# All rows behind the convolution turned by VectorE and DRAM in a two-layer streaming encoder

## The chip, the cores and the metric

The kernel runs on one core of a Trainium2 chip. The core has TensorE (PE in the profile, with its weight loads as PEld), VectorE (DVE), ScalarE (ACT), GpSimd (POOL) and SyncE (SP), which here issues the DMAs. The metric is the time of one execution on the device in microseconds (us), as the median of several runs. Instructions of one engine run in the order that was fixed when the program was built; engines wait for each other through semaphores.

## The reference: what is computed

The input is 256 rows (time steps) of 1024 float32 channels, h below. There are two layers. Each is a macaron: half a SwiGLU feed-forward network (FFN), a mixer, half an FFN again, each added to h; a last RMSNorm follows. The mixer of the first layer is a convolution module, that of the second is latent attention. What matters here is the end of the convolution and the FFN behind it:

```python
u = a * jax.nn.sigmoid(b)                  # a, b: the two halves of h @ w_pw1
u = causal_depthwise_conv(u, w_dw)         # 31 taps for each channel
u = jax.nn.silu(rmsnorm(u, g_norm))
h = h + u @ w_pw2                          # 1024 x 1024: "the last products"
h = h + 0.5 * swiglu_ffn(rmsnorm(h, ffn_norm2[0]), w1, w3, w2)
```

## The kernel before, in words

**Tiles and blocks.** The 256 rows are two row blocks tb of 128; the 1024 channels are eight tiles k or f of 128. Weights come in blocks of 1 MB, 128 x 2048 float32, in the order of use. Each is loaded into one of three raw buffers by SP (`load`, lines 162 to 192, and `raw_to`, line 156, which issues loads ahead without casting). It is then split in two pieces of 128 x 1024 each: ACT writes the high part `hi` (line 188), DVE the rest `lo` (line 189), both in the rounded format that TensorE multiplies fast. Five pairs of `hi` and `lo` buffers exist. A product of high precision is three products: high by low, high by high, low by high (`mm3`, lines 272 to 278). The stationary operand of a product is a tile of activations with the channels on the partitions, so h, which lies with the rows on the partitions, has to be turned, scaled by the gain of the norm and split into `Xh` and `Xl` ahead of each FFN. The factor of the norm itself is applied behind the product.

**Two ways of turning.** In the first, TensorE transposes 128 x 128 squares into PSUM, four at a time (`transposed`, line 315), ACT scales them into `Xh` (line 333) and DVE makes `Xl` (line 337); `Norm.part` (line 382) calls it. In the second, `turn_blocks` (line 345) lets DVE transpose the 32 x 32 blocks of 128 x 512 values, SP writes them to DRAM with four DMAs and reads them back with one, and `Norm.columns` (line 430) makes `Xh` and `Xl` from what came back:

```python
last_turn[0] = nc.vector.transpose(t[:, :w], src.rearrange("p (t j q) -> p j t q", t=n, q=32))
d = dram.tile([P, w], F32, tag=tag + "d", name=uid(tag + "d"), bufs=4)
dv = d.rearrange("(j p) (i c) -> i p j c", p=32, c=32 * n)
for i in range(4):
    dma = nc.sync.dma_start(dv[i], t[32 * i:32 * i + 32, :w].rearrange("p (j c) -> p j c", j=4))
...
last_read[0] = nc.sync.dma_start(b[:, :w], d)
```

A `Norm` made with `turn_by_dma` takes the second way for its second row block: `begin` (line 416) issues the turns of h[1], `end` (line 443) the columns, and the FFN starts with `first_chunk` (line 678), whose products go in the order: first half of the chunk for row block 0 (24 products), four k of the second half for row block 0 (12), first half for row block 1 (24), then the rest. The norm behind the convolution is made without it and takes the first way for all 16 squares.

**The end of the convolution** (`conv_in`, from line 776). The tap sums of the last two channel tiles are finished by DVE, ACT and POOL; `ends` (line 993) adds them and squares them (ACT); TensorE sums the squares over the channels; `normed` (line 938) makes the factor (ACT, then POOL's power), spreads it by a small product `rb`, and then for five groups of tiles makes z (DVE, line 954, lists `zs`), `Zh` (ACT, line 958, `zhs`) and `Zl` (DVE, line 960, `zls`). For each list, entries 0 to 4 (or 0 to 7 for `zs`) belong to row block 0 and the rest to row block 1. The last products (`mm`, line 1031) run over tb, then f, then the two output halves d of 512 columns; behind each tb the outputs are added to h (`add`, line 1078, DVE). h[0] is turned by TensorE between the products of tb 1 (line 1114), h[1] between the first products of the FFN (line 1122).

**What sets the order.** A planner orders each engine's instructions by priority and by a simulated time line. `urgent` raises the priority of what a function issues. `order(a, b)` puts a behind b, without a wait on data. `casts[n, i]` are the two casts of piece i of block n; `n_used[0]` is at this place the index of the first weight block of the next FFN. `turns` holds the reads of turned rows; a weight load that is issued later is put behind the last of them (line 183).

Of the kernel before, what the change touches and what calls it, by code (L numbers as in the profile page):

```python
# [23 lines left out]
KT = D // P  # L24
# [15 lines left out]
RAW_BUFS = 3  # L40
W_BUFS = 5
WARM = 21
PIECES = 2
# [41 lines left out]
def trunk(ctx: ExitStack, tc: tile.TileContext, x, xt, first, pos, invf, gfin, wdw,  # L85
# [27 lines left out]
    conv_block = {}  # L113
# [18 lines left out]
    loaded = []  # L132
    n_used = [0]
# [3 lines left out]
    def order(ins, first):  # L137
        tc.add_manual_dep(ins.ins, first.name, mybir.DependencyInfo(
            mybir.DependencyClass.NoSync, mybir.DependencyReason.DATA), reason="order")
# [7 lines left out]
    casts = {}  # L147

    turns = []
    last_read = [None]  # L150
    last_turn = [None]
# [4 lines left out]
    def raw_to(last):  # L156
        while len(loaded) + len(raws) < last:
            src = blocks[len(loaded) + len(raws)]
            raw = rawp.tile([P, HB], F32, tag="raw", name=uid("raw"))
            raws[len(loaded) + len(raws)] = raw, nc.sync.dma_start(raw[:, :src.shape[-1]], src)  # L160
# [66 lines left out]
    h = [const.tile([P, D], F32, name=f"h{tb}") for tb in range(NT)]  # L227
# [15 lines left out]
    for k in range(KT):  # L243
        c = slice(k % 4 * 512, k % 4 * 512 + 512)
# [42 lines left out]
    def tbs(tb):  # L287
        return slice(tb * P, (tb + 1) * P)
# [56 lines left out]
    def turn_blocks(pool, src, n, tag, after=()):  # L345


        w = n * P
        t = pool.tile([P, 512], F32, tag=tag + "t", name=uid(tag + "t"), bufs=2)
# [5 lines that stand above are left out]
            for a in after:  # L355
                order(dma, a.ins)
        b = pool.tile([P, 512], F32, tag=tag + "b", name=uid(tag + "b"), bufs=2)
        last_read[0] = nc.sync.dma_start(b[:, :w], d)
        return b[:, :w].rearrange("p (i t q) -> p t i q", i=4, q=32)

    class Norm:


        def __init__(self, gname, half=False, turn_by_dma=None):
            self.col = GCOL[gname]
            self.half = half

            self.pool = turn_by_dma
            self.turning = []

            self.first_ahead = False
            self.whole = False
            self.xh = xp.tile([P, KT, S], F32R, tag="Xh", name=uid("Xh"))
            self.xl = xp.tile([P, KT, S], F32R, tag="Xl", name=uid("Xl"))
            self.r = [None] * NT
            self.rh = [None] * NT
            self.turned = ()
            self.lows, self.highs = [], []

            self.between = None  # L380
# [34 lines left out]
        @urgent  # L415
        def begin(self):

            raw_to(len(loaded) + RAW_BUFS)
            first = [dma for raw, dma in raws.values()]
            for q in range(2):  # L420
                self.turning.append(turn_blocks(self.pool, h[1][:, 512 * q:512 * q + 512], 4, "h", first))
                first = [last_read[0]]
                turns.extend(first)
                if self.first_ahead and q == 0:
                    order(last_turn[0], self.lows[3].ins)
                    for low in self.lows[4:]:
                        order(low, last_turn[0].ins)
# [165 lines left out]
    class Rows:  # L593
# [4 lines left out]
        def mm(self, part, i, tb, d, o, f0, f1, o0=0, o1=512, after=(), after_last=()):  # L598
            hi, lo = part
            for j in range(2):  # L600
                f = 2 * i + j
                c = slice(j * D + d * 512 + o0, j * D + d * 512 + o1)
                mm = mm3(o, self.zh[:, f, tbs(tb)], self.zl[:, f, tbs(tb)], hi[:, c], lo[:, c], f == f0,
                         f == f1 - 1, [*after, *after_last] if j else after)
            return mm
# [166 lines left out]
    def conv(X, make_next):  # L772
        with tc.tile_pool(name="conv", bufs=1) as act:
            return conv_in(act, X, make_next)

    def conv_in(act, X, make_next):
# [49 lines left out]
        mm = None  # L826
        for n, (i, tb) in enumerate(CONV_STEPS):
            t = every if tb is None else tbs(tb)
            load_to(conv_block[CONV_TILES[min(CONV_TILES.index(i) + 2, KT - 1)]] + 1)
            gate, u = bank("A", "gate"), bank("A", "u")  # L830
            mm = products(i, 1, t, gate, mm)
            if n == 1:
                X.late((mm,))
                mm = X.turned[-1]
            mm = products(i, 0, t, u, mm)
# [19 lines left out]
        mm = products(7, 1, tbs(1), last_gate, mm)  # L855
# [3 lines left out]
        mm = pairs(mm)  # L859
# [57 lines left out]
        sq = {}  # L917

        def square(k, t):
            if k not in sq:  # L920
                sq[k] = act.tile([P, S], F32, tag="sq", name=uid("sq"), bufs=8)
            return nc.scalar.activation(sq[k][:, t], Y[:, k, t], AF.Square)
# [11 lines left out]
        zs, zhs, zls, norms = [], [], [], []  # L934
# [58 lines left out]
        def ends(tb, after):  # L993

            t = tbs(tb)

            @urgent
            def add():
                for k in CONV_LAST:
                    if CONV_HALVES[k, tb] < TAPS:  # L1000
                        last = nc.vector.tensor_add(Y[:, k, t], part[k][:, t], Y[:, k, t])
                        order(last, dve_ends[-1].ins if tb == 0 else dve_last[-4 if k == CONV_LAST[0] else -1].ins)
                        if tb == 0:
                            firsts_of["add"] = last
                        elif k == CONV_LAST[1]:

                            order(zls[4], last.ins)
                    firsts_of["sq"] = square(k, t)
                sums[tb] = sums_of(tb, CONV_LAST, after)

            add()
# [19 lines left out]
        def mm(f, tb, d, kinds="lhx"):  # L1031
            w = loaded[conv_block[-1 - f // 2]]
            c = slice(f % 2 * D + d * 512, f % 2 * D + d * 512 + 512)
            hi, lo = w
            for n, kind in enumerate(kinds):
                p = nc.tensor.matmul(o[tb, d], (Zl if kind == "x" else Zh)[:, f, tbs(tb)],  # L1036
                                     (lo if kind == "l" else hi)[:, c], start=(f, kind) == (0, "l"),
                                     stop=(f, kind) == (KT - 1, "x"))
                if kind == "l":
                    firsts.append(p)  # L1040
            return p
# [15 lines left out]

        for ins in dve_first[-4:]:
            order(ins, firsts_of["add"].ins)
        order(prods_last[-16], firsts_of["sq"].ins)  # L1060
        ms_ins, power = norms[0]
        order(power, pool_last[-22].ins)
        for ins in pool_last[-21:]:
# [13 lines left out]
        @urgent  # L1077
        def add(tb, d):
            c = slice(d * 512, d * 512 + 512)
            last = nc.vector.tensor_add(h[tb][:, c], o[tb, d], h[tb][:, c])  # L1080
            if tb == 0:
                order(last, zls[7].ins)

        nxt = None
        n_used[0] = max(conv_block.values()) + 1
# [1 line left out]
        for tb in range(NT):  # L1087
            for d in range(2 * tb):
                o[tb, d] = bank("A", "o")
            for f in range(KT):  # L1090
                firsts.clear()

                for kinds in ("lhx",) if f > 1 else ("x",) if (tb, f) == (0, 0) else ("lh", "x"):
                    now = [mm(f, tb, d, kinds) for d in range(2)]
                if tb == 0 and f == 1:
                    sums_of(1, early[5:], now[1])
                elif tb == 0 and f == 5:
                    then = now[1]
                elif tb == 0 and f == 6:

                    ends(1, then)
                    for p in firsts:
                        order(p, sums[1].ins)
                    normed(1, (now[1],))
                elif tb == 0 and f == 7:
                    for p in firsts:
                        order(p, brow[1].ins)

                    for i in range(PIECES):
                        hi, lo = casts[max(conv_block.values()) + 1, i]  # L1110
                        order(hi, zhs[7].ins)
                        order(lo, zs[-1].ins)
                if tb == 1 and f in (2, 4):
                    nxt.part(0, f // 2 - 1, (now[1],))
                if tb == 1 and f == 4:
                    nxt.rms(0)
            for d in range(2):
                add(tb, d)
            if nxt is None:
                nxt = make_next(act)  # L1120
                nxt.between = []
        nxt.part(1, 0)
        return nxt


# [342 lines left out]
    X = ffn(X, lambda act: Plain("mix_0", act), beside)  # L1468
    for _ in todo:
        pass  # L1470
    X = conv(X, lambda act: Norm("ffn2_0", half=True))
    apart.close()
    X = ffn(X, lambda act: Norm("ffn1_1", half=True, turn_by_dma=rows), apart=True)
    X = ffn(X, lambda act: Norm("mix_1", turn_by_dma=rows), apart=True)
# [99 lines left out]
```

## Time and profile before

| | |
|---|---|
| median of 3 runs | 917.44 us (917.42 to 917.92) |
| the profiled execution's own time | 916.85 us |
| its span, first to last instruction | 915.0 us |
| granted TensorE clock, mean | 0.999 |
| DVE busy, ACT busy | 593.0 us (65%), 494.7 us (54%) |
| q1, SP's DMAs | 194.32 MB, 61.5% of 16 DMA engines' span |
| end of the convolution to the next FFN's second chunk | from 265.86 to 300.59 us of the span |

How to read it: times in the profile count from the first instruction of the span. A line of the time line has the start, the length, the engine, the line of the kernel, the operation, what is written and read (buffer numbers left out), the shape and the number of instructions merged in it; in square brackets stands the idle time before it and what ended that. Busy time of TensorE is modelled from pipelined products whose lengths overlap, so the distance between two starts says more than a length.

### The profile page before, as it was taken

Reading aid. Unit: us, or ns where it says so; the run is one execution under the profiler, and the core shown is the slowest. Engines: PE = TensorE matmul, PEld = TensorE weight load, DVE = VectorE, ACT = ScalarE, POOL = GpSimd, SP = SyncE. Lnnn points to the kernel's source line nnn. Section 1 sums busy time; section 2 is a strip of 40 time slices with the busy share of each in tenths; the row PEclk is TensorE's granted clock in tenths of the full one; section 3 lists DMA queues with packets and bytes.
Section 4 is the critical chain, followed back from the end, with each engine's and each line's share of the span. In section 5 each row is a group of like instructions: output and inputs, shape, how many; then the busy total and the mean of one; then the engine's idle time right before and its main releaser. Section 6 shows DMA issues by size and latency. Waiting matters only on the chain.

```text
span 915.0 us, 12095 instructions
## 1 busy us (share of the span) xinstructions
PE 908.0 (99%) x4329; PEld 764.0 (83%) x4329; DVE 593.0 (65%) x934; ACT 494.7 (54%) x845; POOL 125.8 (14%) x259
## 2 busy tenths in 40 slices
PE   9999999999999999999999999999999999999997
PEld 7888888898988888888888888888898888888886
DVE  6885764489987666654476666545768577566633
ACT  7654544388877444543374544433677564454432
POOL 1730000079941000000010000000400010000000
PEclk9999999999999999999999999999999999999999
DMA  9987776533227766776568777755445378776711
GB/s 338 319 290 257 254 275 226 187 140 138 93 79 272 247 230 236 248 232 225 196 208 283 249 246 241 238 205 159 167 145 184 140 250 301 242 245 223 254 47 47
DMA packets 66732, 195.78 MB, mean 214 GB/s; under 512 B 11888, under 2 KB 38384, under 8 KB 47344
## 3 DMA queue, kind: packets, MB, share of 16 engines
q1 hardware_dynamic: 66240, 194.32, 61.5%
q8 instruction: 34, 0.56, 0.2%
q10 hardware_dynamic: 432, 0.69, 0.2%
q14 instruction: 26, 0.21, 0.1%
HBM read 180.30 MB, written 14.68 MB: 213 GB/s over the span
## 4 chain that ended last, share of the span: by engine, by line
PE 99%; DMA 0%; ACT 0%; SPq 0%; DVE 0%; issue 0%; ACTq 0%
PE u L274 17%; PE u L278 17%; PE u L277 17%; PE o L278 10%; PE o L274 10%; PE o L277 10%; PE u L801 3%; PE gate L801 3%; PE o L1036 2%; PE u L283 2%; PE tp L318 1%; PE pairs L844 1%; PE a L277 1%; PE a L274 1%; PE a L278 1%; PE nope L277 1%
## 5 line engine op out<-in xcount | busy, mean ns | idle before, releaser
L189 DVE TENSOR_TENSOR lo<-raw,hi 128x1024 fp32r<-128x1024 f32 (+1 forms) x292 | 344.4, 1220 | 177.2 <-ACT hi L188 176.6
L188 ACT CAST hi<-raw 128x1024 fp32r<-128x1024 f32 x294 | 292.1, 1046 | 241.7 <-PE o L278 81.9
L274 PE MATMUL u<-lo,Xh 128*128 128x512 f32 x672 | 261.7, 389 | 0.0
L278 PE MATMUL u<-hi,Xl 128*128 128x512 f32 x672 | 261.6, 389 | 0.0
L277 PE MATMUL u<-hi,Xh 128*128 128x512 f32 x672 | 261.5, 389 | 0.0
L278 PEld LDWEIGHTS u<-hi,Xl 128*128 128x128 f32 x672 | 126.1, 188 | 26.8 <-DVE Xl L337 0.5
L277 PEld LDWEIGHTS u<-hi,Xh 128*128 128x128 f32 x672 | 126.1, 188 | 26.0
L274 PEld LDWEIGHTS u<-lo,Xh 128*128 128x128 f32 x672 | 126.1, 188 | 26.0
L278 PE MATMUL o<-hi,Gl 128*128 128x512 f32 (+1 forms) x356 | 137.7, 387 | 0.0
L277 PE MATMUL o<-hi,Gh 128*128 128x512 f32 (+1 forms) x356 | 137.7, 387 | 0.0
L274 PE MATMUL o<-lo,Gh 128*128 128x512 f32 (+1 forms) x356 | 137.3, 387 | 0.0
L309 POOL TENSOR_TENSOR ms<-ss 128x1 f32<-128x1 f32 x16 | 9.4, 589 | 590.7 <-ACT junk L301 590.7
L278 PEld LDWEIGHTS o<-hi,Gl 128*128 128x128 f32 x356 | 66.8, 188 | 13.6
L277 PEld LDWEIGHTS o<-hi,Gh 128*128 128x128 f32 x356 | 66.9, 188 | 13.5
L274 PEld LDWEIGHTS o<-lo,Gh 128*128 128x128 f32 x356 | 66.9, 188 | 13.5
L675 ACT CAST Gh<-gb 128x512 fp32r<-128x512 f32 (+1 forms) x48 | 28.0, 583 | 70.8 <-DMA gb<-gd 70.8
L676 DVE TENSOR_TENSOR Gl<-gb,Gh 128x512 fp32r<-128x512 f32 (+1 forms) x48 | 31.3, 652 | 53.5 <-ACT Gh L675 53.5
L890 DVE SCALAR_TENSOR_TENSOR acc<-V,dw,acc 128x128 f32<-128x128 f32 (+1 forms) x174 | 53.9, 392 | 0.0
L911 ACT ACTIVATE prod<-V,dw 128x128 f32<-128x128 f32 (+1 forms) x128 | 45.6, 415 | 1.9 <-POOL Y L912 1.0
L763 DVE TENSOR_TENSOR s<-s,u 128x512 f32<-128x512 f32 (+1 forms) x48 | 30.5, 635 | 7.9 <-PE u L278 7.9
L762 ACT ACTIVATE s<-u,R 128x512 f32<-128x512 f32 (+1 forms) x48 | 31.1, 649 | 4.6 <-PE u L278 3.9
L350 DVE STREAM_TRANSPOSE gt<-s 128x512 f32<-128x512 f32 (+1 forms) x48 | 32.0, 666 | 1.4
(225 smaller groups left out, 884.8 us busy)
## 6 DMA issues: line engine op xcount, KB each, us to landing
raw<-in_f2w SPq DMA_DIRECT2D x66, 1024.0 KB, 5.0
raw<-in_f1w SPq DMA_DIRECT2D x62, 1024.0 KB, 5.1
raw<-in_cw SPq DMA_DIRECT2D x12, 1024.0 KB, 4.8
gd<-gt SPq DMA_DIRECT2D x160, 64.0 KB, 3.3
gb<-gd SPq DMA_DIRECT2D x40, 256.0 KB, 4.4
raw<-in_wo SPq DMA_DIRECT2D x4, 1024.0 KB, 4.8
raw<-in_wuq SPq DMA_DIRECT2D x3, 1024.0 KB, 4.8
raw<-in_f1w SPq DMA_DIRECT2D x8, 256.0 KB, 4.7
```

What stands on the lines that cost most here:

```text
L188: casts[len(loaded), i] = (nc.scalar.copy(hi[:, c], raw[:, c]), low.tensor_sub(lo[:, c], raw[:, c], hi[:, c].bitcast(F32)))
L189: low.tensor_sub(lo[:, c], raw[:, c], hi[:, c].bitcast(F32)))
L274: mm = nc.tensor.matmul(o, ah, bl, start=start, stop=False)
L277: nc.tensor.matmul(o, ah, bh, start=False, stop=False)
L278: return nc.tensor.matmul(o, al, bh, start=False, stop=stop)
L350: last_turn[0] = nc.vector.transpose(t[:, :w], src.rearrange("p (t j q) -> p j t q", t=n, q=32))
L676: nc.vector.tensor_sub(Gl[:, f, tbs(tb)].rearrange("p t (i q) -> p t i q", q=32), bv, gh.bitcast(F32))
L762: nc.scalar.activation(s[:, :w], u[0, tb][:, :w], AF.Silu, scale=X.r[tb])
L763: nc.vector.tensor_mul(s[:, :w], s[:, :w], u[0, tb][:, w:] if both else u[1, tb])
L801: mm = nc.tensor.matmul(u[:, t], w[:, c], X.x[:, k, t], start=(k == 0), stop=(k == KT - 1))
L890: dve_last.append(nc.vector.scalar_tensor_tensor(out if j == j1 - 1 else y, v, w, y, op0=ALU.mult, op1=ALU.add))
L911: prods_last.append(nc.scalar.activation(p, v, AF.Copy, scale=w))
```

## The change

The norm behind the convolution is made with `turn_by_dma`, so none of its rows are turned by TensorE. h[0] is added and turned as soon as each output of tb 0 is there, in a stated order between DVE's other work; `Norm.both` marks this norm, and for it `begin` issues only one weight load ahead, behind the reads of h[0], and puts the low parts of h[0] behind the turns of h[1]. The last products of tb 1 go over f 0 to 3 for both outputs, then f 4 to 7 for output 0, then f 4 to 7 for output 1. The two high casts of the first weight block of the next FFN are put behind the first square and behind the factor's first step of row block 1, its first low cast in front of z, its second behind the last `Zl`.

```diff
@@ class Norm, __init__
+            self.both = False
@@ class Norm, begin
-            raw_to(len(loaded) + RAW_BUFS)
+            raw_to(len(loaded) + (1 if self.both else RAW_BUFS))
             first = [dma for raw, dma in raws.values()]
+            if self.both:
+                for dma in first:
+                    order(dma, turns[-1].ins)
             for q in range(2):
                 self.turning.append(turn_blocks(self.pool, h[1][:, 512 * q:512 * q + 512], 4, "h", first))
                 first = [last_read[0]]
                 turns.extend(first)
+                if self.both:
+                    for low in self.first_lows[q]:
+                        order(low, last_turn[0].ins)
@@ conv_in, ends: firsts_of["sq"] becomes a list of the two squares
-                    firsts_of["sq"] = square(k, t)
+                    firsts_of.setdefault("sq", []).append(square(k, t))
...
-        order(prods_last[-16], firsts_of["sq"].ins)
+        order(prods_last[-16], firsts_of["sq"][1].ins)
@@ conv_in, add
             if tb == 0:
-                order(last, zls[7].ins)
+                order(last, (zls[6], zs[-1])[d].ins)
+                nxt.first_turns.append(turn_blocks(nxt.pool, h[0][:, c], 4, "h"))
+                turns.append(last_read[0])
+                for ins in ((zls[7], zs[-4]), zls[8:])[d]:
+                    order(ins, last_turn[0].ins)
@@ conv_in, the last products
-            for f in range(KT):
+            halves_of = [(f, (0, 1)) for f in range(KT - 4 * tb)]
+            halves_of += [(f, (d,)) for d in range(2 * tb) for f in range(KT - 4, KT)]
+            for f, ds in halves_of:
                 firsts.clear()
                 for kinds in ("lhx",) if f > 1 else ("x",) if (tb, f) == (0, 0) else ("lh", "x"):
-                    now = [mm(f, tb, d, kinds) for d in range(2)]
+                    now = [mm(f, tb, d, kinds) for d in ds]
+                if ds == (1,):
+                    for p in firsts:
+                        order(p, half_done.ins)
+                if tb == 1 and f == KT - 1:
+                    add(1, ds[0])
+                    half_done = now[0]
...
+                    (hi, lo), (hi2, lo2) = (casts[n_used[0], i] for i in range(PIECES))
+                    order(hi, firsts_of["sq"][0].ins)
+                    order(firsts_of["sq"][1], hi.ins)
+                    order(hi2, norms[1][0].ins)
+                    order(zhs[5], hi2.ins)
+                    order(lo, zls[4].ins)
+                    order(zs[8], lo.ins)
+                    order(lo2, zls[9].ins)
                     for i in range(PIECES):
-                        hi, lo = casts[max(conv_block.values()) + 1, i]
-                        order(hi, zhs[7].ins)
-                        order(lo, zs[-1].ins)
-                if tb == 1 and f in (2, 4):
-                    nxt.part(0, f // 2 - 1, (now[1],))
-                if tb == 1 and f == 4:
-                    nxt.rms(0)
-            for d in range(2):
-                add(tb, d)
-            if nxt is None:
+                        hi, lo = casts[n_used[0] + 1, i]
+                        order(hi, zhs[9].ins)
+                        order(lo, lo2.ins)
+            if tb == 0:
                 nxt = make_next(act)
-                nxt.between = []
-        nxt.part(1, 0)
+                nxt.both = True
+                nxt.first_turns, nxt.first_lows = [], [[], []]
+                for d in range(2):
+                    add(0, d)
+                for q in range(2):
+                    for high, low in nxt.columns(nxt.first_turns[q], q, 0):
+                        order(high, casts[n_used[0] + 2, PIECES - 1][0].ins)
+                        order(low, casts[n_used[0] + 1, PIECES - 1][1].ins)
+                        nxt.first_lows[q].append(low)
+                    if q == 1:
+                        for i in range(PIECES):
+                            order(casts[n_used[0] + 2, i][1], low.ins)
+                nxt.rms(0)
@@ trunk
-    X = conv(X, lambda act: Norm("ffn2_0", half=True))
+    X = conv(X, lambda act: Norm("ffn2_0", half=True, turn_by_dma=rows))
```

More of the change, by code (lines that the diff above doesn't have):

```diff
@@ L995, in ends @@
             t = tbs(tb)
+            firsts_of["sq"] = []
             @urgent
```

## The prediction

> **What bounds the kernel now.** I read the page first: the span, the busy time of TensorE (PE) and the shares of the chain that ended last.
>
> ```profile
> span 915.0 us, 12095 instructions
> PE 908.0 (99%) x4329; PEld 764.0 (83%) x4329; DVE 593.0 (65%) x934; ACT 494.7 (54%) x845; POOL 125.8 (14%) x259
> PE 99%; DMA 0%; ACT 0%; SPq 0%; DVE 0%; issue 0%; ACTq 0%
> ```
>
> TensorE is the bound from end to end; nothing else holds a share of the chain. So only two things count: how much PE time the change takes out, and whether PE is made to wait anywhere. I went next to the timeline of PE from the first product of the convolution's second row block (265.86) to the first product of the next FFN's second chunk (300.59).
>
> ```profile
> 265.86 0.39 PE L1036 MATMUL o<-lo,Zh 128*128 128x512 f32 x1
> ...
> 271.12 0.39 PE L1036 MATMUL o<-hi,Zl 128*128 128x512 f32 x1
> 271.35 0.60 PE L318 MATMUL tp<-ident,h 128*128 128x128 f32 x4
> 271.70 0.47 PE L1036 MATMUL o<-lo,Zh 128*128 128x512 f32 x1
> ...
> 280.62 0.39 PE L278 MATMUL u<-hi,Xl 128*128 128x512 f32 x1
> ...
> 300.59 0.39 PE L274 MATMUL u<-lo,Xh 128*128 128x512 f32 x1
> ```
>
> ```profile
> L318 PE MATMUL tp<-ident,h 128*128 128x128 f32 x16 | 2.4, 276 | 0.0
> L1080 DVE TENSOR_TENSOR h<-o,h 128x512 f32<-128x512 f32 x4 | 2.6, 680 | 0.0
> ```
>
> The durations overlap, so the starts are what to read. From 265.86 to 271.12 lie 23 steps, 0.2287 us each; from 280.62 to 300.59 lie 88, 0.2269 us each. Four transposes push the next product from 271.35 to 271.70, though the row gives each 276 ns.
>
> **What the change takes off PE.** The stretch is 300.59 - 265.86 = 34.73 us and holds 48 products of the convolution, 96 of the FFN and the 16 transposes of h. Without the transposes, and with every operand there in time, it is 48 x 0.2287 + 96 x 0.2269 = 10.98 + 21.78 = 32.76. So 1.97 us is all there is to win (0.123 us for each transpose, a short wait for h included). Doing the last products output by output only reorders them and costs PE nothing.
>
> The rest of the sum is whether the rows come in time over the longer way: an add and a 32x32 turn on VectorE (DVE), four DMAs to DRAM, one back, then the scaled high part on ScalarE (ACT) and the low part on DVE. I name the four next weight blocks B0 to B3 and start the FFN at 265.86 + 10.98 = 276.84.
>
> **The moved casts.** B0's casts now stand in front of and between the convolution's last copies.
>
> ```profile
> 262.10 0.31 ACT L922 ACTIVATE sq<-Y 128x128 f32<-128x128 f32 x1 [1.18 <-DVE Y L1001]
> 265.05 0.31 ACT L958 ACTIVATE Zh<-z 128x128 fp32r<-128x128 f32 x1 [1.84 <-DVE z L954]
> 264.67 1.12 DVE L954 SCALAR_TENSOR_TENSOR z<-Y,G,rb 128x128 f32<-128x128 f32 x4 [2.26 <-PE rb L947]
> 265.71 0.58 DVE L960 TENSOR_TENSOR Zl<-z,Zh 128x128 fp32r<-128x128 f32 x2
> 266.20 1.12 DVE L954 SCALAR_TENSOR_TENSOR z<-Y,G,rb 128x128 f32<-128x128 f32 x4
> 268.77 2.35 DVE L189 TENSOR_TENSOR lo<-raw,hi 128x1024 fp32r<-128x1024 f32 x2
> 271.04 0.75 DVE L960 TENSOR_TENSOR Zl<-z,Zh 128x256 fp32r<-128x256 f32 x2
> 271.15 28.00 SPq L180 DMA_DIRECT2D raw<-in_f2w  x8
> 272.73 1.99 ACT L188 CAST hi<-raw 128x1024 fp32r<-128x1024 f32 x2
> ```
>
> The two waits of ACT (1.18 and 1.84) each take one high cast of 1.99 / 2 = 1.0, and DVE's 2.26 takes one low cast of 2.35 / 2 = 1.18. All three go at nothing; without that cover each would be added to the norm on which PE waits. If the first cast ran 0.2 us over its wait, the square and the norm behind it would be late by that much, but PE then has products of the first row block to do, so up to about 0.3 us stays hidden.
>
> **DVE's own order.** After the second low part of Z (265.71 + 0.58 = 266.29) it has to do: add 0.68, turn 0.71, four scalings 1.12, a low part 0.4, add 0.68, turn 0.71, two low parts 0.75, B0's second low cast 1.18, B1's two 2.35. That is 8.58, so 274.9 at the latest; consecutive rows overlap by 0.05 us (266.20 begins before 266.29), which makes it about 274.5. Z's low parts move by about a microsecond (the third from 267.7 to 268.9), and PE wants that one 16 steps behind 265.86, at 269.5: still in time. The first turn ends at 267.6, the second at 270.3.
>
> The durations of the turn and the new low and high parts are those of the same code in the next FFN:
>
> ```profile
> 451.81 0.71 DVE L350 STREAM_TRANSPOSE rows<-h 128x512 f32<-128x512 f32 x1
> 465.10 1.24 DVE L439 SCALAR_TENSOR_TENSOR Xl<-rows,G,Xh 128x128 fp32r<-128x128 f32 x4 [0.16 <-ACT Xh L438]
> 464.66 1.28 ACT L438 ACTIVATE Xh<-rows,G 128x128 fp32r<-128x128 f32 x4 [0.73 <-DMA rows<-hd]
> ```
>
> The four old Xh and Xl groups go, four new ones of 1.28 and 1.24 come; DVE gains four turns (2.84 us), which its idle time behind 276 holds.
>
> **The DRAM trips.** SyncE (SP) issues in order, so a read that waits for its writes holds what is behind it. The same trips stand in the trace:
>
> ```profile
> 451.14 0.33 SPq L160 DMA_DIRECT2D raw<-in_f1w  x1
> 452.55 1.75 SPq L354 DMA_DIRECT2D hd<-rows  x4
> 457.20 0.34 SPq L358 DMA_DIRECT2D rows<-hd  x1
> 457.64 1.83 SPq L354 DMA_DIRECT2D hd<-rows  x4
> 461.21 0.34 SPq L358 DMA_DIRECT2D rows<-hd  x1
> 462.46 1.84 SPq L354 DMA_DIRECT2D hd<-rows  x4
> 465.70 0.34 SPq L358 DMA_DIRECT2D rows<-hd  x1
> 468.31 1.28 ACT L438 ACTIVATE Xh<-rows,G 128x128 fp32r<-128x128 f32 x4 [1.79 <-DMA rows<-hd]
> 641.43 1.75 SPq L354 DMA_DIRECT2D hd<-rows  x4
> 645.76 0.34 SPq L358 DMA_DIRECT2D rows<-hd  x1
> ```
>
> From first write to read: 3.24 (462.46), 3.57 right behind another read (457.64), 4.33 (641.43), 4.65 with a weight load 1.4 us ahead (452.55; 6.06 from that load). From read to ACT's start: 2.61 (465.70 to 468.31) to 3.45 (461.21 to 464.66). The DMA engines are free when the change begins to use them (columns of the view by stages: busy PE, PEld, DVE, ACT, POOL, then clock, DMA share, GB/s):
>
> ```profile
> 268.00:270.00 2.00, 2.00 (x11) 1.63 (x10) 2.00 (x4) 2.00 (x6) 0.00 (x0) 1.00 0.04 8
> 270.00:272.00 2.00, 2.00 (x12) 1.69 (x11) 2.00 (x4) 2.00 (x4) 0.00 (x0) 1.00 0.00 0
> ```
>
> So: h0's first half writes 267.6, reads 270.8, reaches ACT at 273.5 to 274. ACT has B2's high casts before it, which end at 272.73 + 1.99 = 274.7 in the old order and hardly earlier in the new one, since the same product frees their buffer; so it starts at about 275. PE wants the first column at 276.84. Margin over 1 us. Second half: writes 271.2, reads 274.8, ACT at 277.5 to 278.2; wanted at 276.84 + 12 x 0.2269 = 279.56. Margin 1 us. B3's load follows at 275.2 (in the old order loads began at 271.15). h1's first half: its last product starts at 276.84 - 13 x 0.2287 = 273.9 and ends 0.39 later, DVE is free at 274.6, add and turn end at 276.0, the writes queue behind B3, the read comes 6.06 after that load at 281.2, ACT at 284.0; wanted after 36 products at 285.0. Second half: writes 281.6, reads 285.2 (3.57), ACT 287.8 (2.61), first column 0.3 later at 288.1; wanted after 48 products at 287.7. **This is the tight place.** With the quickest rows throughout (3.24 each) it is 0.3 us early, with the slowest (4.33, 3.45) 1.6 late. DVE's low parts of h0 stand behind the turns of h1, which end at 276.0 and 278.6 (the last output is there at 277.0, then add and turn): first at 276.3 and 278.9, wanted by the third product of their column at 277.3 and 280.0. Behind a high part that waits on ACT stand B3's casts, wanted after 60 products at 290.5, and behind a waiting low part on DVE B2's, wanted after 24 at 282.3 and there by about 281.2. B4's load, now behind h1's read at 285.6, is wanted at 276.84 + 96 x 0.2269 = 298.6; with 5 us to land and 2.4 for its casts it has 5 us to spare.
>
> For the wait at the tight place I take 0.1 us of the range -0.3 to 1.6 (less than nothing brings nothing): in this stretch only B3 is on the queues, as quiet as beside the quick rows. Sum: 1.97 - 0.1 = 1.9 us. The profiled execution took 916.85 for its span of 915.0, so it would take 914.95; the median of the runs, 917.44, is 0.59 above it, and the forecast for that is **915.5** (0.21% faster). 0.2%, or 1.83 us, is about what a measurement here can tell from no change, so the forecast stands just across that line.
>
> One page speaks against this change. The Trainium skill, "VectorE: DVE Perf Modes", section "Rules for kernel authors", gives TensorE as the place for a 128x128 transpose whose result may lie in PSUM, as it may here. By that rule the DRAM way loses, which is the second rival below; no run yet shows it for this stage.
>
> **Rivals.**
>
> (1) *h1's trips become the wait.* For it: 288.1 against 287.7 by middle rows. Against it: the quick rows. Price with the slow rows 1.6, at most 3.6 if DVE's order also goes wrong (a low part behind the second turn is 1.4 late): 915.4 + 1.6 = 917.0, range 915.9 to 919.0.
>
> (2) *Slower: the trips run at the loaded rate.* The same kind of trip for G in the loaded stages has these landings:
>
> ```profile
> gd<-gt SPq DMA_DIRECT2D x160, 64.0 KB, 3.3
> gb<-gd SPq DMA_DIRECT2D x40, 256.0 KB, 4.4
> hd<-rows SPq DMA_DIRECT2D x32, 64.0 KB, 2.4
> rows<-hd SPq DMA_DIRECT2D x8, 256.0 KB, 2.8
> ```
>
> A write is 0.9 and a read 1.6 longer. The last column of h1 hangs on four writes and one read in a row, 4 x 0.9 + 1.6 = 5.2, so 915.4 + 5.3 = 920.7. It decides against the change once the links together lose 3.8 us. For it: everything is on one queue, with B3 in the middle. Against it: a DMA share of 0.00 to 0.04 beside the first trips.
>
> (3) *Each transpose costs PE its duration.* 16 x 0.276 = 4.4 us would go: 913.1. Against it: four of them moved the next product by 0.35 only. The Trainium skill, "TensorE: Matmul & The Clock Gate", section "Part 4: PE-mode transpose", has about 275 ns for one in a kernel; taken as a price that would be this rival, an estimate of 4.4 us.
>
> (4) *The early add isn't early*: the planner leaves it behind other work of DVE, such as the 2.35 of two low casts, the tight place comes 2 us late and eats all: 917.4.
>
> **How the numbers follow.** Forecast 0.55 (own range 915.2 to 916.1, across the line: 0.43 faster, 0.12 same); rival 1 0.18 (0.16 same, 0.02 slower); rival 2 0.20, slower; rival 3 0.04, faster; rival 4 0.03, same. Together faster 0.47, same 0.31, slower 0.22. The range leaves out rivals 2 and 3 and most of the far end of rival 1: 914.9 to 918.0.
>
> **What would show it.** Right: no transposes of h between 265 and 280, the distance between the same two products near 32.8 us, a cast of B0 in each of the three waits, the first high part from DRAM on ACT before 276, the last group of h1 near 287.5. Wrong: a step in PE's starts ahead of the FFN's first product (h0 late), ahead of its 13th (h0's second half), its 37th or its 49th (h1), or at 298 (weights). The forecast fails if the second trip of h1 is over half a microsecond late, or if the planner's new order costs PE time elsewhere.

## The result, and the profile after

| | before | changed |
|---|---|---|
| median of 12 runs of each, side by side | 917.2 us (916.75 to 918.79) | 919.05 us (918.25 to 922.4) |
| ratio | | 1.0023, 95% interval 1.0015 to 1.003 |
| profiled execution, its span | 916.85, 915.0 us | 918.93, 917.2 us |

The changed kernel is 0.23% slower. The forecast was 915.5, the range 914.9 to 918.0, so the time is outside it, on the other side of no change.

The page of the changed kernel: the busy times, the costliest product, the code packets and the shares of the chain that ended last.

```profile
PE 907.0 (99%) x4313; PEld 762.5 (83%) x4313; DVE 596.0 (65%) x938; ACT 495.5 (54%) x845; POOL 126.8 (14%) x259
...
q8 instruction: 34, 0.56, 0.2%
...
PE 96%; DMA 2%; DVE 1%; ACT 0%; SPq 0%; issue 0%; ACTq 0%
...
L274 PE MATMUL u<-lo,Xh 128*128 128x512 f32 x672 | 261.9, 390 | 2.4 <-ACT Xh L447 2.4
```

The 16 products of TensorE's transposes are gone (4329 to 4313) and its busy time fell by 1.0, yet the span grew by 2.2. The chain says where: TensorE had 99% of it, and now DMA and DVE hold 3%. The last row names the place: products of the FFN waited 2.4 us for `Xh`. The time line of PE shows the two waits:

```profile
266.04 0.39 PE L1046 MATMUL o<-lo,Zh 128*128 128x512 f32 x1
...
277.03 0.40 PE L274 MATMUL u<-lo,Xh 128*128 128x512 f32 x1
...
285.10 0.39 PE L278 MATMUL u<-hi,Xl 128*128 128x512 f32 x1
287.03 0.50 PE L274 MATMUL u<-lo,Xh 128*128 128x512 f32 x1 [1.54 <-ACT Xh L447]
...
289.66 0.39 PE L278 MATMUL u<-hi,Xl 128*128 128x512 f32 x1
290.87 0.50 PE L274 MATMUL u<-lo,Xh 128*128 128x512 f32 x1 [0.83 <-ACT Xh L447]
...
301.92 0.39 PE L274 MATMUL u<-lo,Xh 128*128 128x512 f32 x1
```

The FFN's first product comes 277.03 - 266.04 = 10.99 us behind the reference product, as forecast (10.98). The 37th and the 49th come late. From one product's start to the next it is 0.23 us when the operands are there, so the two steps of 1.93 and 1.21 lose 1.70 and 0.98, 2.68 in all. The whole stretch is 301.92 - 266.04 = 35.88 us, against 34.73 before and 32.86 forecast. Behind it nothing more changes on TensorE: the end of the stretch is 1.33 us later than before, and the last product 1.32.

SyncE's time line of the changed kernel shows why h1 was late. Each group of four writes and the read behind it is one trip.

```profile
267.85 1.78 SPq L354 DMA_DIRECT2D hd<-rows  x4
272.72 0.34 SPq L358 DMA_DIRECT2D rows<-hd  x1
273.16 1.81 SPq L354 DMA_DIRECT2D hd<-rows  x4
276.70 0.34 SPq L358 DMA_DIRECT2D rows<-hd  x1
277.14 0.38 SPq L160 DMA_DIRECT2D raw<-in_f2w  x1
277.57 1.97 SPq L354 DMA_DIRECT2D hd<-rows  x4
283.71 0.34 SPq L358 DMA_DIRECT2D rows<-hd  x1
284.11 1.87 SPq L354 DMA_DIRECT2D hd<-rows  x4
287.67 0.34 SPq L358 DMA_DIRECT2D rows<-hd  x1
```

The first trip takes 4.87 us with no data transfer ahead of it, where 3.2 was forecast; the one behind B3's load is read 6.57 us after that load, not 6.06. The other two (3.54 and 3.56) are as forecast.

What happens in the first trip stands in the view by stages (columns as in the prediction) and in the DMA view of the one microsecond from 270 to 271:

```profile
269.00:270.00 1.00, 1.00 (x6) 0.82 (x5) 0.96 (x3) 1.00 (x5) 0.00 (x0) 1.00 0.66 137
270.00:271.00 1.00, 1.00 (x6) 0.83 (x5) 1.00 (x3) 1.00 (x3) 0.00 (x0) 1.00 0.41 83
271.00:272.00 1.00, 1.00 (x7) 0.80 (x6) 1.00 (x2) 1.00 (x2) 0.00 (x0) 1.00 0.04 4
```

```profile
q8 instruction: 1, 0.02, 8.6%
```

Among the writes' packets lies one of an instruction queue: 16 KB, 8.6% of 16 engines for 1 us, so 1.37 us on one DMA engine. The trace has it from 270.10 to 271.47. All packets of the writes but nine have moved by 270.6; the nine move from 271.45 to 271.93, one after the other (the row with 4 GB/s), as the share of one engine that was held up. Without them the writes would have landed 1.3 us earlier. A code packet was there in the kernel before as well, at 269.37, and it was the only packet of any kind from 262 to 272 (DMA view of before):

```profile
DMA packets 1, 0.02 MB, mean 2 GB/s; under 512 B 0, under 2 KB 0, under 8 KB 0
...
q8 instruction: 1, 0.02, 0.8%
```

So the packet hardly moved: it comes 3.5 us behind the reference product before and 4.1 after. What is new is the awaited write that now stands there.

The rest of the loss is behind the last product, whose rows are, first before, then changed:

```profile
908.87 0.28 PE L278 MATMUL o<-hi,Gl 128*128 128x256 f32 x1
```

```profile
910.19 0.28 PE L278 MATMUL o<-hi,Gl 128*128 128x256 f32 x1
```

Of the span, 6.16 and 6.96 us lie behind its start: 0.8 more, which no wait of TensorE explains.

### The profile page after: what moved, and what is told of

Its sections match the earlier page's. It is cut to its first block, busy times and chain, and to the rows that moved or that the text cites. A ratio compares the mean times of both kernels' runs of the same rounds, so it can differ in the third digit from the quotient of the medians.

```text
span 917.2 us, 12102 instructions
## 1 busy us (share of the span) xinstructions
PE 907.0 (99%) x4313; PEld 762.5 (83%) x4313; DVE 596.0 (65%) x938; ACT 495.5 (54%) x845; POOL 126.8 (14%) x259
## 4 chain that ended last, share of the span: by engine, by line
PE 96%; DMA 2%; DVE 1%; ACT 0%; SPq 0%; issue 0%; ACTq 0%
PE u L278 16%; PE u L274 16%; PE u L277 16%; PE o L278 10%; PE o L277 10%; PE o L274 10%; PE u L810 3%; PE gate L810 3%; PE u L283 2%; PE o L1046 1%; PE tp L318 1%; DMA rows<-hd 1%; DMA hd<-rows 1%; PE pairs L853 1%; PE a L278 1%; PE a L277 1%
## 5 line engine op out<-in xcount | busy, mean ns | idle before, releaser
L309 POOL TENSOR_TENSOR ms<-ss 128x1 f32<-128x1 f32 x16 | 6.7, 421 | 590.8 <-ACT junk L301 590.8
L921 POOL TENSOR_TENSOR odd<-odd,prod 128x128 f32<-128x128 f32 (+1 forms) x62 | 33.7, 547 | 0.4 <-ACT prod L920 0.3
```

The source lines that it names most:

```text
L921: pool_last.append(nc.gpsimd.tensor_tensor(o, o, p, op=ALU.add))
```

## The experiments

The kernel before, run beside these, had medians of 917.03 us (runs 1 to 4) and 917.01 us (runs 5 to 8).

**1. h1's columns made from something that isn't awaited.**

```diff
-            for both in self.columns(self.turning[q], q, 1):
+            for both in self.columns((self.first_turns if self.both else self.turning)[q], q, 1):
```

> The columns of row block 1 are made from the turned rows of row block 0 (so the second row block is computed from the wrong rows); the trips of h1 still run, but nothing waits for them. Instructions and their order on every engine are those of the changed kernel. Theory A, the two waits of TensorE for h1's rows (1.7 and 1.0 us by the steps in its starts, with about 0.3 us of slower starts behind them) are the whole loss: 919.05 - 3.0 = 916.1 us, ratio to before about 0.999, and no step in TensorE's starts at the 37th and 49th product of the FFN. Rival B, a good part of the loss lies elsewhere (the new order on DVE and ACT, later stages, the last output writes, which were 0.8 us longer in the profile after): 917.0 to 918.5 us.

Measured: 919.17 us, ratio 1.0017 (1.0008 to 1.0026), waits of 2.2 us. The experiment missed its aim: the turned halves of h1 land in the same two buffers as those of h0, so the columns wait for the same reads, and the program behaves as the changed kernel again. It serves as a repeat of it.

**2. B3's load behind all trips.** The load, its casts and the products that want it come behind h1's columns:

```diff
-            raw_to(len(loaded) + (1 if self.both else RAW_BUFS))
-            first = [dma for raw, dma in raws.values()]
+            raw_to(len(loaded) + (0 if self.both else RAW_BUFS))
+            first = turns[-1:] if self.both else [dma for raw, dma in raws.values()]
...
-                        order(ins, cast.ins)
+                        if self.both:
+                            order(cast, ins.ins)
+                        else:
+                            order(ins, cast.ins)
...
+            if X.both:
+                groups[3:] = [(1, 1, range(4)), (1, 0, range(4, 8)), (1, 1, range(4, 8))]
```

> B3's load goes behind h1's second read instead of ahead of h1's first writes, its casts behind h1's columns, and the FFN's first chunk takes k 0 to 3 of row block 1 before the products that need B3. Theory A (what makes h1 late is the row of trips with B3's load in its middle): h1's first trip takes 3.6 us from write to read instead of 6.1, both waits go, 915.3 to 916.2 us, ratio 0.998 to 0.999. Rival C, the trips are late on their own (the first one took 4.9 us with nothing ahead of it): the first wait goes, the second stays at about 1 us, 917 us. Rival B: 918 us or more.

Measured: **916.08 us, ratio 0.9988 (0.9979 to 0.9996)**, below both kernels, by a margin over the kernel before that the interval only just sets apart from none, and within what theory A expected. SyncE's time line of this kernel:

```profile
267.63 1.78 SPq L354 DMA_DIRECT2D hd<-rows  x4
272.36 0.34 SPq L358 DMA_DIRECT2D rows<-hd  x1
...
276.63 1.88 SPq L354 DMA_DIRECT2D hd<-rows  x4
280.50 0.34 SPq L358 DMA_DIRECT2D rows<-hd  x1
```

The first trip is as long as in the changed kernel (4.73), but h1's two take 3.87 and 3.62 (the last read at 284.52) and their reads come 3.2 us earlier than there. TensorE waits nowhere in the stretch, which is 32.91 us long, and its last product comes 1.88 us earlier than before, of 1.97 that the transposes cost. So what the change takes off TensorE is worth what was forecast, and the trips with the load between them are what eats it.

**3. One small write of SyncE ahead of the first trip**, 64 KB to a place that nothing reads:

```diff
                     ends(1, then)
+                    scratch = dram.tile([P, P], F32, tag="scratch", name="scratch")
+                    nc.sync.dma_start(scratch, Y[:, 7, tbs(1)])
```

> One extra 64 KB write to another DRAM tile is issued when the last Y is there, at about 262.3 us, some 5 us ahead of h0's first writes; the rest is the changed kernel. Theory C, the first trip is long because the queues had stood idle for some 16 us: its time from first write to read falls from 4.9 to 3.2 to 3.6 us, all later trips come about 1.4 us earlier, the waits for h1 shrink by as much, 917.6 us. Rival (first use of this DRAM tile, or the trip is simply that long): 4.9 us again and 919.0 us.

Measured: 918.29 us, ratio 1.0012 (1.0004 to 1.0021). The first trip still takes 4.97 us (267.95 to 272.92), h1 is waited for as before and TensorE ends 1.25 us later than before. So the first trip isn't long because the queue was idle; that theory falls. The time is nevertheless 0.8 us below the changed kernel's, nearly all of it behind the last product (6.38 us in place of 6.96). The DMA view of both kernels from 912 to 918 (GB/s in slices of 0.15 us), first the changed kernel:

```profile
GB/s 0 0 0 0 0 0 0 0 0 96 328 341 424 328 396 355 341 307 369 157 27 27 21 27 7 0 0 0 0 0 0 0 0 0 0 0 0 0 0 0
...
q14 instruction: 1, 0.01, 0.8%
```

and the one with the early write:

```profile
GB/s 0 0 0 0 0 0 0 0 0 232 328 294 376 369 382 396 375 307 328 110 0 0 0 0 0 0 0 0 0 0 0 0 0 0 0 0 0 0 0 0
```

In the changed kernel an 8 KB packet of another instruction queue lies among the packets of the last output (0.77 us, from 3.73 us behind the last product), and a trickle of 21 to 27 GB/s follows: again the share of one engine. The output's last packet lands 5.49 us behind the last product, in place of 4.87 before. One more instruction on SyncE moved the code packet to 0.22 us behind the last product, ahead of the output's data; the trickle is gone, and the last packet lands at 4.88. So the packet is a block of SyncE's code. The other runs bear this out: with 729 records of SyncE in the trace (run 2) the packet comes 6.39 us behind the last product, with 731 or 732 (the changed kernel and runs 1, 4 and 7) at 3.7 to 4.2, with 733 or 734 (runs 3 and 5) at 0.2 or sooner, and with 738 (run 8) ahead of that product. The kernel before has 701 and no such packet there; the change, which adds SyncE's DMAs, had moved one into the last output.

**4. B3's load between h1's two trips.**

```diff
                 first = [last_read[0]]
                 turns.extend(first)
+                if self.both and q == 0:
+                    raw_to(len(loaded) + 1)
+                    for raw, dma in raws.values():
+                        order(dma, first[0].ins)
+                    first = [dma for raw, dma in raws.values()]
```

> B3's load moves one place on SP: behind h1's first read, ahead of h1's second writes. Theory A (the last read returns when four trips and one load have gone through one queue in a row, whatever their order): the first wait goes, the second grows from 1.0 to about 2.7 us, 919.0 us as the changed kernel. Rival (a load costs only where it stands ahead of the first trip; the last one makes it up): both waits shrink, 917 us.

Measured: 923.45 us, ratio 1.0068 (1.0054 to 1.0082), far from what either theory said. The waits and, by stages, what the clock did (the column behind POOL):

```profile
PE u L274 <- ACT Xh L449: 3.4, 1, 3.4
```

```profile
288.00:290.00 2.00, 1.22 (x2) 0.50 (x2) 2.00 (x4) 1.66 (x6) 0.00 (x0) 0.54 0.97 279
290.00:292.00 2.00, 1.95 (x5) 1.58 (x6) 1.83 (x7) 1.09 (x4) 0.00 (x0) 0.50 1.03 430
...
294.00:296.00 2.00, 2.00 (x8) 1.58 (x7) 1.91 (x2) 1.45 (x3) 0.00 (x0) 0.76 1.03 434
```

The edit left h1's columns ordered behind B3's casts. Its first high part therefore waited on ACT not for its own read (280.34) but for B3 (cast at 286.30, column at 288.19). And behind that wait the granted clock was about half for 6 us. The run says nothing on the two theories, only what a long wait costs here: the stretch is 39.74 us against 32.91 in run 2, which is 6.8 more: 3.6 by the late step itself and 3.3 by the slow products behind it. The Trainium skill, "TensorE: Matmul & The Clock Gate", section "Part 1: The HAM clock gate (the "warmup" mystery)", has the clock halved after an idle window of about 3.4 us; this trace agrees, 0.50 behind a wait of 3.4, and no drop behind the waits of 1.5 in the changed kernel.

**5. TensorE's code block moved out of the first trip.** Twice as many warm-up products of half the width at the kernel's start: the same columns and 42 more instructions, so that each block of TensorE's code loads earlier in the work.

```diff
-            mm = nc.tensor.matmul(b[:, :256], still[:, :P], still, start=True, stop=True)
+            mm = nc.tensor.matmul(b[:, :w], still[:, :P], still[:, :w], start=True, stop=True)
...
-    keep_warm(WARM)
+    keep_warm(2 * WARM, w=128)
```

> The changed kernel with 42 warm-up products of 128 columns at its start in place of 21 of 256: the same columns, 42 more instructions for TensorE (a weight load and a product each), so that each 16 KB block of TensorE's code (256 instructions) is loaded some 4 to 5 us earlier in the work. Theory A: h0's first trip of 4.87 us is a trip of about 3.55 and 1.3 us in which one DMA engine carries a 16 KB packet of the instruction queue (it starts at 269.97 and takes 1.37 us, between the writes' packets; the last of the 80 small packets that close the write and its neighbours lands at 271.79, all others by 270.48). With that packet near 265.3, before the write, the trip takes 3.4 to 3.7 us; the second read, B3's load and h1's first read each come 1.0 to 1.4 us earlier, and the waits for h1's first and fifth groups fall from 1.5 and 0.8 us to below 0.4 together; the end of TensorE's work comes 2.0 to 2.9 us earlier; time 916.2 to 917.2. Rival B: the first trip is long by itself (first use of that place in DRAM, an idle queue), and the packet beside it is chance: trip 4.7 to 5.0, waits of 2 to 2.6 us, time 918.6 to 919.4. Rival C: the trip gets shorter, but h1's trip doesn't, since the load's bytes fill the engines: waits of 1.5 us or more, time 918.0 to 918.8.

**6. The same edit in the kernel before**, as a control:

> The kernel before with the same 42 warm-up products. In the kernel before the 16 KB packet at 269.25 lies between trips: no data packet is in flight from 257 to 272. Theory A, and every other one that gives the code's place no weight of its own: within 0.4 us of the kernel before (ratio 0.9996 to 1.0004), first trip of h1 as before. If the narrower warm-up products themselves change the time (a later or colder start), it shows here as a difference of 0.5 us or more, and the run of the changed kernel with them is to be read against this one.

Measured: 917.13 us, ratio 0.9996 (0.9987 to 1.0005), for the changed kernel with it, and 917.6, ratio 1.0003 (0.9994 to 1.0012), for the kernel before with it. SyncE's time line, the code packet (from the DMA view of 267 to 269) and PE's waits of the changed kernel with moved code:

```profile
268.52 1.78 SPq L354 DMA_DIRECT2D hd<-rows  x4
271.69 0.34 SPq L358 DMA_DIRECT2D rows<-hd  x1
...
276.14 0.36 SPq L160 DMA_DIRECT2D raw<-in_f2w  x1
276.62 2.00 SPq L354 DMA_DIRECT2D hd<-rows  x4
282.67 0.34 SPq L358 DMA_DIRECT2D rows<-hd  x1
```

```profile
q8 instruction: 1, 0.02, 2.8%
```

```profile
PE u L274 <- ACT Xh L447: 0.8, 1, 0.8
```

With the packet ahead of the write's data (267.81, 0.89 us) the first trip takes **3.17 us in place of 4.87**. In the seven kernels with the change that have the packet among that data, it takes 4.50 to 5.16. The stretch is 34.07 us, 1.8 shorter than in the changed kernel. The warm-up costs something of its own: in the control the time and all of TensorE are 0.6 later than before, past the mark of 0.5, though the stretch there is 34.71 as ever. So the two are to be read against each other: 917.13 to 917.6, TensorE's end 0.41 earlier in the changed kernel. Theory A is right on the trip and on the time, and too hopeful on the waits: it had less than 0.4 left, and one of 0.8 at the 49th product stays. Rival C is right that the trip behind the load gets no shorter (B3's load to h1's read still takes 6.53), but not on the waits of 1.5 or the time of 918.0 or more that it expected.

**7. The last products for both outputs together, as before.**

```diff
-            halves_of = [(f, (0, 1)) for f in range(KT - 4 * tb)]
-            halves_of += [(f, (d,)) for d in range(2 * tb) for f in range(KT - 4, KT)]
+            halves_of = [(f, (0, 1)) for f in range(KT)]
```

> The changed kernel with the last products of h1 for both outputs together, as before, and both adds at the end. h1's first half is then turned at about 278.4 in place of 275.9. If SyncE's order decides (h1's first write is issued at 277.57, behind B3's load at 277.14, whenever the turn is done before), the write comes 0.8 to 1.0 us later and the first wait grows by as much: time 919.7 to 920.2. Rival: the bytes of B3's load, which fill the engines until about 281, are in front of the write anyway: the trip ends as before, time within 0.3 of the changed kernel's 919.05. A third: the wait grows past 3 us and the granted clock falls as in the run with the load between: 921 or more.

Measured: 919.34 us, ratio 1.0019 (1.0009 to 1.0028): as the changed kernel. The waits and SyncE's time line:

```profile
PE u L278 <- DVE Xl L448: 1.2, 1, 1.2
PE u L274 <- ACT Xh L447: 1.1, 2, 0.8
```

```profile
277.19 0.38 SPq L160 DMA_DIRECT2D raw<-in_f2w  x1
278.34 1.76 SPq L354 DMA_DIRECT2D hd<-rows  x4
283.52 0.34 SPq L358 DMA_DIRECT2D rows<-hd  x1
```

h1's write is issued 0.77 us later than in the changed kernel and read 0.19 earlier. So behind B3's load it is the load that sets the read, not when the write is issued; without the load ahead of it (run 2) the same trip takes 3.87 us from its own first write, in place of 6.14. In exchange DVE's low part of h0 comes behind the adds and the first turn of h1, and the FFN's third product waits 1.2 for it; the waits for h1 shrink by as much. Output by output is therefore worth 1.2 us on DVE, which the trip behind the load takes back.

**8. B3's load last, and eight small writes of SyncE in the norm's wait**, as in 3, to move its code block:

```diff
+                    for i in range(8):
+                        nc.sync.dma_start(scratch[16 * i:16 * i + 16], Y[16 * i:16 * i + 16, 7, tbs(1)])
```

> The kernel with B3's load last (916.08, ratio 0.9988 to the kernel before) and eight small writes of 8 KB by SyncE in the norm's wait, to a place that nothing reads: 8 more instructions of SyncE, so that its code block, which loaded at the very end of the work in every kernel with the turn in DRAM (6.39 us after the last product here, 3.7 to 4.2 in the others, where it lies between the packets of the last output write), is loaded before the last product. Theory A: the 0.7 us by which the tail behind the last product is longer than before (6.86 against 6.16) falls to 0.3 or less; time 915.3 to 915.8. Rival: the tail is long for another reason, 6.7 to 7.0 again; time 916.0 to 916.3. If the small writes disturb h0's first trip, it shows as a first trip over 5 us and a wait of TensorE.

Measured: **915.74 us, ratio 0.9983 (0.9974 to 0.9992)**, the fastest of all. No code packet lies behind the last product, and what lies behind that product is 6.49 us, against 6.86 in run 2. Theory A had expected 0.3 or less above the 6.16 of before, and the time that it named; 0.33 stays, so it just misses on the first and holds on the second.

## Why the prediction was wrong, step by step

**Right.** *What bounds the kernel, and what is to be won:* 1.97 us for 16 transposes; with B3's load last TensorE ends 1.88 earlier. That is 0.12 us for each, so rival 3's 275 ns is not what one costs this kernel, as it was not by the starts of before. *The moved casts cost nothing:* on ACT's time line of the changed kernel they stand in the waits of the square and of the norm.

```profile
261.01 1.04 ACT L188 CAST hi<-raw 128x1024 fp32r<-128x1024 f32 x1
262.30 0.31 ACT L931 ACTIVATE sq<-Y 128x128 f32<-128x128 f32 x1 [0.24 <-DVE Y L1011]
...
263.29 1.04 ACT L188 CAST hi<-raw 128x1024 fp32r<-128x1024 f32 x1
265.24 0.31 ACT L967 ACTIVATE Zh<-z 128x128 fp32r<-128x128 f32 x1 [0.90 <-DVE z L963]
```

*DVE's order, h0 in time, the FFN's start:* no step ahead of the 1st product, 0.08 at the 13th. *The place:* the two steps are at the 37th and the 49th, which I had named.

**Wrong: the prices of two links in the chain of trips.** ACT's time line has the high parts of h1 that came back:

```profile
286.57 1.28 ACT L447 ACTIVATE Xh<-rows,G 128x128 fp32r<-128x128 f32 x4 [1.91 <-DMA rows<-hd]
...
290.42 1.28 ACT L447 ACTIVATE Xh<-rows,G 128x128 fp32r<-128x128 f32 x4 [1.99 <-DMA rows<-hd]
```

h1's first high part was forecast at 284.0, 1.0 us ahead of its product, and came at 286.57. Of the 2.57 us, 1.94 stand already at B3's load (277.14 for 275.2): the first write 0.25 late and the first trip 1.67 too long. 0.57 come from the load to the read (6.57 for 6.0), 0.06 from there to ACT. The wait that I put at 0.1 us, all of it at the 49th product, became 2.68, of which 1.70 at the 37th, where I had put nothing; starts that were slower right behind the waits added 0.4; all of TensorE stood 0.18 later even ahead of the change, and what lies behind the last product grew by 0.8. That makes the 4.0 us between 914.95 and 918.93.

- *The first trip, 3.2.* The failed sentence is "in this stretch only B3 is on the queues, as quiet as beside the quick rows". I had looked for data. Runs 3, 5 and 6 show what it was: not the idle queue, but a block of TensorE's code on one DMA engine; 1.7 us go with it when it is moved, 0.4 more than the packets behind it were late. The trace of before had said so, in a row that I quoted: the slow quiet trip of 4.33 us at 641.43 has the same packet in it. The DMA view of before from 641 to 646:

```profile
GB/s 0 0 0 0 33 33 33 197 197 262 295 426 205 287 275 246 213 254 188 189 209 156 156 217 111 29 8 8 8 16 21 20 21 16 0 0 0 0 0 0
...
q8 instruction: 1, 0.02, 1.2%
```

  The same trickle follows it. I took the difference between 3.24 and 4.33 for scatter, where it had a cause that could be placed: a code packet stood at 269.37 in the trace of before, in the middle of the write that I forecast from 267.6 to 270.8. The Trainium skill, "Runtime: NRT & Kernel Launch", section "Instruction fetch mechanics", has code loaded in blocks of 256 instructions on DMA queues of its own, at a cost mostly hidden. The blocks agree (2 x 4313 records in 34 packets are 254 each); hidden they are from the engine that runs the code, not from a transfer whose last packet is awaited.
- *B3's load to h1's read, 6.06.* It was 6.57 here and 6.33 to 6.67 in the other five kernels that have the load just ahead of a trip of h1. The row that gave 6.06 had nothing in front of the load; here the read of h0's second half, 256 KB, is issued 0.44 ahead of it. That this read makes the half microsecond is only argued. That the load sets the read was shown by run 7, and that the waits go when the load is out of the way by run 2.
- *The slow end of the range, "1.6 late".* "0.3 us early" comes out only with the quick rows in every trip, 1.6 only with the slow ones in h1's last trip alone. And 1.6 is by how much that trip gets slower, not how late it is: 288.1 becomes 289.7, 2.0 behind the 287.7 at which it is wanted. With 4.33 in all the trips that the forecast put at 3.2, 3.6 and 3.57, and 3.45 from read to ACT, h1's first half comes at 286.5, 1.5 late, and its second at 291.6, 3.9 late. Measured were 286.57 and 290.42 (on ACT), so the prediction's own slow rows, carried through the whole chain, came near the result.
- *Behind the last product* I had nothing. Some 0.6 of the 0.8 us are SyncE's code block in the last output (run 3); the rest stays open: 0.2 to 0.3 in the three kernels with these trips whose last output has no code packet among or behind it (6.38, 6.48 and 6.49 against 6.16). So does why run 2 has 6.86, where the output's data had all landed at 4.87 and the packet comes at 6.39; with that packet gone (run 8) it is 6.49.

**The rivals.** Rival 1 is what happened: h1's trips became the wait. The time is just past the far end of its own range (919.0), which it reached not by DVE's order going wrong, as that end supposed, but by longer trips and 0.8 us of another kind. The overall range had left that end out. Rival 2 gave the sign, but its mechanism isn't there: two trips ran at 3.54 and 3.56, and from read to ACT it took 2.6 to 2.9. Rival 4 isn't either: the adds of h0 stood in their place (266.39 and 269.08), and run 7 shows that the place of h1's adds hardly matters behind the load. The rule of the Trainium skill that the prediction named ("VectorE: DVE Perf Modes", section "Rules for kernel authors", a 128x128 transpose on TensorE) does not decide this stage, where TensorE is the bound. With the load out of the way the DRAM way is 0.12% faster than the kernel before (run 2, interval 0.04 to 0.21%), and the changed kernel loses by the load and the code, not by the way.

## What to carry to other kernels

Where a chain of small transfers must land in time, look for instruction packets beside it in the DMA view, and when the rows of one kind of trip differ by a microsecond, find out why before choosing among them. A change in an engine's number of instructions shifts the places at which its code blocks load, as runs 3, 5 and 8 show, and this can help or hurt by 0.6 to 1.7 us where a transfer is awaited, at the very end of a kernel too. A large load that is wanted late goes behind the small trips that are wanted soon, with its casts and products.

## What the runs showed of the hardware that I had not expected

- A code block of 16 KB holds one DMA engine for 0.9 to 1.8 us (all runs), and an awaited write of 256 KB on all engines was read 1.7 us later for it (4.87 us from write to read, against 3.17).
- SyncE's code block, 8 KB and 0.3 to 0.8 us, among the last output's packets: the span goes on for 7.0 to 7.2 us behind the last product in four kernels, for 6.4 to 6.5 in three where it comes earlier.
- One wait of TensorE of 3.4 us was followed by some 6 us at about half the clock, which cost 3.3 us more.
